# Issuing the first load of a streaming Lp-pooling kernel from the ScalarE queue instead of the SyncE queue

## The chip, the cores and the metric

The kernel runs on one core of one Trainium2 chip. The metric is the device time of one execution in microseconds (us); medians over several executions are given. A profile is one execution taken by the hardware profiler. Its span is about 2 us shorter than the device time, and its clock starts with the span. Engines are ACT (ScalarE), DVE (VectorE) and SP (SyncE, which here only issues DMAs); "the DMA engines" are the core's 16 engines that move the bytes.

## The reference

```python
batch, channels, length = 32, 256, 4096      # float32, p = 2, kernel_size = 4
for i in range(out_length):                  # out_length = length // 4
    window = np.abs(x[:, :, 4*i:4*i+4]) ** p
    result[:, :, i] = np.mean(window, axis=-1) ** (1.0 / p)
```

With p = 2, each output is the square root of the mean of four squares. The kernel reads 134.22 MB and writes 33.55 MB, and does very little arithmetic per byte.

## The kernel before

The input is cut into 32 blocks of 128 partitions x 8192 columns (4.19 MB each). For each half block ACT squares in place, DVE adds groups of four, and ACT takes the root of the result one step later. There are four input buffers. Three loads are issued ahead of the loop and a fourth at its start; each later load reuses a buffer and so has to wait for the reduces of the block four places ahead of it. Finished outputs leave from the ACT queue in groups of four blocks; two late groups are held back and leave from SP.

```python
in_pool = ctx.enter_context(tc.tile_pool(name="in_pool", bufs=4))

def load(i):
    xt = in_pool.tile([P, W], fp32)
    nc.sync.dma_start(out=xt, in_=x_block(i))
    xts[i] = xt

# ... root(i, c): Sqrt on ACT; after a group's last root, nc.scalar.dma_start of the group

for i in range(3):
    load(i)

pending = None
for i in range(n):                           # n = 32
    if i + 3 < n:
        load(i + 3)
    # ...
    for c in range(0, W, CH):                # two halves of 4096 columns
        xh = xts[i][:, c:c + CH]
        nc.scalar.activation(out=xh, in_=xh, func=mybir.ActivationFunctionType.Square)
        nc.vector.tensor_reduce(out=ots[gi][:, at:at + CH // k], in_=xh.rearrange("p (n j) -> p n j", j=k),
                                axis=mybir.AxisListType.X, op=mybir.AluOpType.add)
        if pending is not None:
            root(*pending)
        pending = (i, c)
```

## Time and profile before

| | before |
|---|---|
| device time, median (first 3 runs) | 395.74 us (395.67 to 395.85) |
| span of the profile | 393.7 us |
| bytes moved, mean rate | 167.79 MB, 426 GB/s |
| ACT busy, DVE busy | 75%, 72% |
| first Square starts | 12.87 us |
| Square of the last block starts | 373.62 us |

From the profile page of the kernel before, three parts: the utilization rows (busy tenths in 40 equal slices of the span, and GB/s), the DMA queues (q1 is SP's, q10 ACT's), and the chain of waits that ended last, by engine.

```profile
DVE  0399996739976399764988559866598846999992
ACT  1699987469883798828988189863998819999981
...
DMA  8999998999999999999999999999999999999997
GB/s 350 446 430 426 426 426 373 449 446 430 433 426 426 426 430 453 440 430 433 426 426 426 426 449 443 427 433 430 426 426 426 443 446 433 430 433 426 426 435 314
...
q1 hardware_dynamic: 4896, 141.56, 83.9%
q10 hardware_dynamic: 1008, 26.21, 15.5%
...
DMA 72%; ACT 17%; DVE 9%; SPq 0%; issue 0%; ACTq 0%
```

The DMA row is the one without gaps. ACT and DVE rest for a quarter of the span, so nothing they do is worth time unless it leaves the DMA engines without work.

The timeline of ACT at the start of the kernel before (start, duration, engine and line, operation; in brackets the idle time before it and what ended it):

```profile
12.87 7.12 ACT L108 ACTIVATE xt<-xt 128x4096 f32<-128x4096 f32 x2 [10.86 <-DMA xt<-in_x_dram]
...
22.57 3.62 ACT L108 ACTIVATE xt<-xt 128x4096 f32<-128x4096 f32 x1 [0.21 <-DMA xt<-in_x_dram]
...
32.28 3.62 ACT L108 ACTIVATE xt<-xt 128x4096 f32<-128x4096 f32 x1 [0.55 <-DMA xt<-in_x_dram]
...
42.00 3.62 ACT L108 ACTIVATE xt<-xt 128x4096 f32<-128x4096 f32 x1 [0.56 <-DMA xt<-in_x_dram]
```

Each block's first Square waits for a load, and the loads come 9.7 us apart. Now SP's timeline for load 4, the first one that must wait for a buffer:

```profile
25.29 0.33 SPq L79 DMA_DIRECT2D xt<-in_x_dram  x1
```

Load 4 is issued at 25.29 us. The load in front of it in the queue, load 3, lands at 42.0 us. I call the difference, 16.7 us, the lead: about that long could the issue come later before the queue ran empty.

### The profile page before, as it was taken

Reading aid. Unit: us, or ns where it says so; the run is one execution under the profiler, and the core shown is the slowest. Engines: PE = TensorE matmul, PEld = TensorE weight load, DVE = VectorE, ACT = ScalarE, POOL = GpSimd, SP = SyncE. Lnnn points to the kernel's source line nnn. Section 1 sums busy time; section 2 is a strip of 40 time slices with the busy share of each in tenths; the row PEclk is TensorE's granted clock in tenths of the full one; section 3 lists DMA queues with packets and bytes.
Section 4 is the critical chain, followed back from the end, with each engine's and each line's share of the span. In section 5 each row is a group of like instructions: output and inputs, shape, how many; then the busy total and the mean of one; then the engine's idle time right before and its main releaser. Section 6 shows DMA issues by size and latency. Waiting matters only on the chain.

```text
span 393.7 us, 357 instructions
## 1 busy us (share of the span) xinstructions
DVE 282.8 (72%) x64; ACT 294.7 (75%) x130; POOL 0.2 (0%) x4
## 2 busy tenths in 40 slices
DVE  0399996739976399764988559866598846999992
ACT  1699987469883798828988189863998819999981
POOL 0000000000000000000000000000000000000000
DMA  8999998999999999999999999999999999999997
GB/s 350 446 430 426 426 426 373 449 446 430 433 426 426 426 430 453 440 430 433 426 426 426 426 449 443 427 433 430 426 426 426 443 446 433 430 433 426 426 435 314
DMA packets 5906, 167.79 MB, mean 426 GB/s; under 512 B 656, under 2 KB 656, under 8 KB 656
## 3 DMA queue, kind: packets, MB, share of 16 engines
q1 hardware_dynamic: 4896, 141.56, 83.9%
q10 hardware_dynamic: 1008, 26.21, 15.5%
q14 instruction: 2, 0.02, 0.0%
HBM read 134.22 MB, written 33.55 MB: 426 GB/s over the span
## 4 chain that ended last, share of the span: by engine, by line
DMA 72%; ACT 17%; DVE 9%; SPq 0%; issue 0%; ACTq 0%
DMA xt<-in_x_dram 72%; ACT xt L108 14%; DVE ot L112 9%; ACT ot L87 2%; SPq L79 0%; ACTq L108 0%
## 5 line engine op out<-in xcount | busy, mean ns | idle before, releaser
L112 DVE TENSOR_REDUCE ot<-xt 128x1024 f32<-128x4096 f32 x64 | 282.8, 4420 | 103.4 <-ACT xt L108 102.6
L108 ACT ACTIVATE xt<-xt 128x4096 f32<-128x4096 f32 x64 | 230.9, 3610 | 87.6 <-DMA xt<-in_x_dram 85.0
L87 ACT ACTIVATE ot<-ot 128x1024 f32<-128x1024 f32 x64 | 67.0, 1047 | 4.2 <-DVE ot L112 3.4
L108 ACT ACT_TABLE_LOAD x1 | 1.3, 1283 | 0.7 <-PEq L139 0.7
L87 ACT ACT_TABLE_LOAD x1 | 1.3, 1283 | 0.0
L139 POOL MEMSET const-uint8-127<- 128x1 uint8 x1 | 0.1, 102 | 0.0
L139 POOL MEMSET const-bfloat16-1.0<- 128x1 bf16 x1 | 0.1, 101 | 0.0
L139 POOL MEMSET const-float32-0.0<- 128x1 f32 x1 | 0.1, 98 | 0.2 <-issue 0.2
L139 POOL MEMSET const-float32-1.0<- 128x1 f32 x1 | 0.1, 98 | 0.0
## 6 DMA issues: line engine op xcount, KB each, us to landing
xt<-in_x_dram SPq DMA_DIRECT2D x32, 4096.0 KB, 35.9
out_dram<-ot ACTq DMA_DIRECT2D x6, 4096.0 KB, 23.2
out_dram<-ot SPq DMA_DIRECT2D x1, 4096.0 KB, 34.1
out_dram<-ot SPq DMA_DIRECT2D x1, 3072.0 KB, 12.3
out_dram<-ot ACTq DMA_DIRECT2D x1, 1024.0 KB, 5.6
```

Source lines behind the costliest of these rows:

```text
L87: nc.scalar.activation(out=o, in_=o, func=mybir.ActivationFunctionType.Sqrt, scale=1.0 / k,)
L108: nc.scalar.activation(out=xh, in_=xh, func=mybir.ActivationFunctionType.Square,)
L112: nc.vector.tensor_reduce(out=ots[gi][:, at:at + CH // k], in_=xh.rearrange("p (n j) -> p n j", j=k), axis=mybir.AxisListType.X, op=mybir. ...
L139: nc = _bacc.Bacc("TRN2", target_bir_lowering=False, num_devices=1)
```

## The change

It puts the first load on another issuing queue. The intent is a quicker head: two sequencers issue in parallel at the start.

```diff
     def load(i):
         xt = in_pool.tile([P, W], fp32)
-        nc.sync.dma_start(out=xt, in_=x_block(i))
+        queue = nc.scalar if i == 0 else nc.sync
+        queue.dma_start(out=xt, in_=x_block(i))
         xts[i] = xt
```

## The prediction

> **What bounds the kernel now.** The DMA engines. The page's utilization rows show them at 90% or more in nearly every one of the 40 slices, 426 GB/s over the span (167.79 MB in 393.7 us), while DVE is busy 72% and ACT 75%. The chain of waits is DMA 72%. Load issues are early: load 4 leaves SP when the reduces of block 0 end, at 25.2 us, while loads 2 and 3 (9.7 us each, read from Squares starting at 12.87, 22.57 us in the timeline) still fill the SP queue until about 42 us. So SP's wait for DVE (293.7 us in the view of waits) costs nothing: there are about 17 us of slack. The last load lands at 373.5 us; two held stores then run under the last block's compute.
>
> **What changes.** No bytes and no work: one of SP's 32 load issues (about 0.4 us each) becomes ACT's first instruction, ahead of its 1.28 us table load. ACT then waits idle until 12.87 us anyway, so that costs nothing. Load 1 now leaves SP at 0.73 us, beside load 0 from ACT, not behind it.
>
> **Consequence.** The Trainium skill, "DMA: Bandwidth & Descriptors", section "Queues, rings and completion order", says that each of the 16 DMA engines goes round-robin between queues. This trace agrees: beside the first store, load 6 took 18.1 us (63.8 to 82.0) instead of 9.7. So loads 0 and 1 each get half the rate, and both land near 22 us. The first Square starts at about 22.5 us (range 20 to 23), not 12.87.
>
> **Critical share.** None of that delay should reach the end. From 22.5 us ACT runs back to back at 2 x (3.6 + 1.06) = 9.3 us a block, against 9.7 a load. Block 0's reduces end near 35 us, so load 4 is issued near 35; load 3 occupies the queue until 42. Load 5 goes near 44.8, before load 4 lands (51.7); load 6 near 54, before 61.5. Slack falls from about 17 to about 7 us but never to zero. The first store moves from 56.4 to about 64.7 us; the longer waits beside it (18 us) let ACT catch up by block 7, at about 91 us. After that the timeline is as before: bytes ahead of load 31 are the same, so it lands at 373.5 and the tail is unchanged. What may move is under 1 us: two queues starting together may fill the opening (the first 13 us moved about 400 GB/s, against 430 later), gaining up to 1 us.
>
> **Predicted:** 395.5 us, 80% range 394.3 to 396.7. Chances: faster by over 2% 0.005, within 2% 0.985, slower by over 2% 0.01.
>
> **What would show it.** Right: first Square near 22 us with Squares of blocks 0 to 3 then back to back; ACT's idle time before the first Square up by about 9.5 us, later idle before Squares down by as much; DMA utilization row unchanged, mean 426 GB/s; last load lands within 1 us of 373.5; SP's issue of load 4 near 35 us. Wrong: first Square near 13 us (no equal sharing), or a hole in DMA between 35 and 65 us (slack ran out), or the last landing moved.
>
> **What would make it wrong.** Unequal arbitration; loads from two queues running together faster or slower than one queue (no two loads on different queues overlap in this trace); the shifted store meeting loads so that a later block finds no load queued.

## The result and the profile after

| | before | after |
|---|---|---|
| device time, median of 6 runs | 395.71 us (395.51 to 395.85) | 395.45 us (395.34 to 395.53) |
| span of the profile | 393.7 us | 393.3 us |
| first Square starts | 12.87 us | 22.85 us |
| load 4 issued | 25.29 us | 35.27 us |
| first store issued | 56.38 us | 63.97 us |
| Square of block 7 starts | 91.64 us | 91.35 us |
| Square of the last block starts | 373.62 us | 373.26 us |

The ratio is 0.9994, with a 95% interval of 0.9981 to 1.0007: the same. A ratio is the mean time of one kernel's fast runs over that of the other's of the same rounds, so it is not quite the ratio of the medians quoted.

The same rows of the page of the changed kernel:

```profile
DVE  0039999995976499764988559866598846999992
ACT  1069999987883798828988189872998819999981
...
DMA  8999999999999999999999999999999999999997
GB/s 340 447 433 433 427 427 403 437 433 433 427 427 427 433 450 437 431 433 430 427 427 427 437 450 433 427 433 430 427 427 430 440 443 433 433 430 430 427 433 317
...
q1 hardware_dynamic: 4752, 137.37, 81.4%
q10 hardware_dynamic: 1152, 30.41, 18.0%
...
DMA 65%; ACT 21%; DVE 11%; issue 0%; ACTq 0%
```

ACT and DVE start a slice later and are then packed with 9s where they had gaps; from about the tenth slice on the digits are almost those of before. The DMA row has changed in a single digit, and 4.19 MB have moved from q1 to q10. ACT's timeline at the start:

```profile
0.73 0.40 ACTq L80 DMA_DIRECT2D xt<-in_x_dram  x1
1.16 1.28 ACT L109 ACT_TABLE_LOAD   x1 [1.16 <-PEq L140]
22.85 7.12 ACT L109 ACTIVATE xt<-xt 128x4096 f32<-128x4096 f32 x2 [20.40 <-DMA xt<-in_x_dram]
...
32.24 3.60 ACT L109 ACTIVATE xt<-xt 128x4096 f32<-128x4096 f32 x1
...
41.30 3.60 ACT L109 ACTIVATE xt<-xt 128x4096 f32<-128x4096 f32 x1
```

The load was issued at 0.73 us, as early as before, and yet the first Square waits 10 us longer. After that the Squares have no bracket: ACT no longer waits for loads, it is behind them. Counting the trace's DMA packets of 32 KB by the microsecond in which they started shows why (these are counts from the trace's DMA records, changed kernel):

```
us from         5   6   7   8   9  10  11  12  13  14
SP queue       10   0  16   0  12   4   1  15   0  15
ACT queue       1  15   0  16   0   5  11   0  16   0
```

The 16 engines take turns between the two queues. Loads 0 and 1 move at half rate each and land together, at 22.83 and 22.65 us. Now the waits of ACT for loads (total, times, longest), first before:

```profile
ACT xt L108 <- DMA xt<-in_x_dram: 85.0, 32, 10.9
```

and after:

```profile
ACT xt L109 <- DMA xt<-in_x_dram: 84.9, 26, 20.4
```

ACT waited for loads as long in total, to 0.1 us. It waited 9.5 us more ahead of the first Square, and six later waits vanished. SP's timeline after, for loads 4 and 5:

```profile
35.27 0.33 SPq L80 DMA_DIRECT2D xt<-in_x_dram  x1
44.78 0.33 SPq L80 DMA_DIRECT2D xt<-in_x_dram  x1
```

Load 3 landed at 42.1 us and load 4 at 51.8 us, so the leads are now 6.8 and 7.0 us. They shrank by the ten microseconds that the head lost, but they did not reach zero, and the DMA engines never noticed.

### The profile page after: what moved, and what is told of

The parts are those of the page before. It is cut to its first block, busy times and chain, and to the rows that moved or that the text cites. A ratio compares the mean times of both kernels' runs of the same rounds, so it can differ in the third digit from the quotient of the medians.

```text
span 393.3 us, 357 instructions
## 1 busy us (share of the span) xinstructions
DVE 282.8 (72%) x64; ACT 294.0 (75%) x130; POOL 0.2 (0%) x4
## 4 chain that ended last, share of the span: by engine, by line
DMA 65%; ACT 21%; DVE 11%; issue 0%; ACTq 0%
DMA xt<-in_x_dram 65%; ACT xt L109 18%; DVE ot L113 11%; ACT ot L88 3%; ACT L88 0%; ACTq L109 0%
## 5 line engine op out<-in xcount | busy, mean ns | idle before, releaser
L109 ACT ACTIVATE xt<-xt 128x4096 f32<-128x4096 f32 x64 | 230.8, 3608 | 87.4 <-DMA xt<-in_x_dram 84.9
```

## The experiments

My theory: the DMA engines bound the kernel; the second queue delays block 0 by 10 us because it lets load 1 share the engines with it; the delay is paid out of the lead of the later loads, and nothing of it reaches the end as long as the lead stays above zero. Rivals: the issuing queue does not matter at all, as the same engines do the work; the delay does cost, but an opening with two queues earns it back; the delay would be made up over the kernel whatever its size; the ACT queue itself is late.

Ten kernels were run, all with correct results. The first four share one chip and the same runs of the kernel before (395.65 us), the next four another call (395.56 us), the last two a third (395.62 us). All diffs are against the kernel before, cut to the lines that matter. I call a difference real where the 95% interval of the ratio leaves out 1.

### The changed kernel again

No edit.

> The changed kernel once more, to be compared on one chip with the three others of this call. Slack theory (DMA engines bound; a late first Square is paid from waiting that ACT and the load queue had to spare): first Square 22.8 us, last load's Square 373.3 us, time 395.4 us, 0.1 to 0.4 us under the kernel before. Rival (the difference between the kernels is noise only): ratio 1.000 within 0.0003.

Measured: 395.58 us, ratio 0.9997 (0.9984 to 1.0009); first Square at 22.83 us, last block's Square at 373.45 us. The first Square repeats to 0.02 us. The gain does not: 0.07 us between the medians here, 0.26 us the first time. So the rival, noise only, stands.

### The same delay with one queue

```diff
-    for i in range(3):
-        load(i)
+    for i in range(3):
+        tile_for(i)                  # buffers in the old order
+    for i in (1, 0, 2):
+        load(i)                      # all on nc.sync
```

> All loads on SP, but load 1 is issued ahead of load 0, so block 0 is as late as in the changed kernel without a second queue. Slack theory: first Square 22.5 us, ACT back to back until block 7, first store near 64 us, time within 0.5 us of the kernel before. Rival (the ten us of delay do cost, and the second queue earns them back): about 405 us. Of the 0.3 us gain: if it comes from where the first store falls, this run is 0.2 to 0.4 us faster than before; if it comes from two queues opening together, it equals the kernel before within 0.1 us.

Measured: 395.41 us, ratio 0.9997 (0.9983 to 1.0011). The first Square starts at 22.48 us and load 4 is issued at 34.90 us. So a delay of 10 us costs nothing without any second queue, and the rival that a second queue earns it back falls. On the 0.3 us question the median alone agrees with "where the first store falls", but the ratio's interval includes 1 and settles nothing.

### Two queues without the delay

```diff
+        if i == 0:
+            for queue, c in ((nc.scalar, 0), (nc.sync, CH)):
+                queue.dma_start(out=xt[:, c:c + CH], in_=x_block(i)[:, c:c + CH])
+        else:
+            nc.sync.dma_start(out=xt, in_=x_block(i))
```

> Load 0 cut into two column halves, one from ACT and one from SP; loads 1 on from SP. Two queues open together as in the changed kernel, but block 0 is not held up by load 1. Sharing theory (what delays block 0 is load 1 running beside it at equal rate): first Square 12.5 to 13.5 us. Rival (a load on the ACT queue lands late by itself): later than 14 us. Time within 0.5 us of before; if the 0.3 us gain comes from two queues opening together it is 0.2 to 0.4 us faster, if from where the first store falls it equals the kernel before within 0.1 us.

Measured: 395.58 us, ratio 1.0 (0.9988 to 1.0013); first Square at 13.05 us. Here ACT issues half of block 0 at 0.73 us and block 0 is on time: what made it late in the changed kernel was not ACT's queue but another load beside it. Opening two queues together gains nothing measurable.

### All four opening loads from ACT

```diff
-        nc.sync.dma_start(out=xt, in_=x_block(i))
+        queue = nc.scalar if i < 4 else nc.sync
+        queue.dma_start(out=xt, in_=x_block(i))
```

> The four opening loads all leave from ACT, the others from SP. In the changed kernel the ACT queue's first packet starts at 3.51 us and the SP queue's at 1.75 us, though both were issued at 0.73 us. If the ACT queue starts late by its nature, the first packet is at 3.5 us, first Square at 14.6 us, and as the DMA engines bound the kernel the time rises by 1.5 to 2 us. If it was late only because SP issued beside it, first packet at 1.75 us, first Square at 12.9 us, time within 0.4 us of before. Sharing theory in both cases: no 22 us landing, although load 0 is on the ACT queue, as nothing runs beside it.

Measured: 397.68 us (396.33 to 398.04), ratio 1.0048 (1.0034 to 1.0062). Half of the expectation held: the ACT queue's first packet starts at 1.75 us and the first Square at 12.81 us, so ACT's queue is not late by nature. The time did not hold: it is 2.0 us over before, and neither theory had said that for an on-time first packet. SP's timeline of this run and ACT's first Squares of blocks 2 and 3 show what began at load 4, the first one from SP:

```profile
25.23 42.96 SPq L80 DMA_DIRECT2D xt<-in_x_dram  x4
...
35.88 3.62 ACT L109 ACTIVATE xt<-xt 128x4096 f32<-128x4096 f32 x1 [4.21 <-DMA xt<-in_x_dram]
...
55.31 3.62 ACT L109 ACTIVATE xt<-xt 128x4096 f32<-128x4096 f32 x1 [10.27 <-DMA xt<-in_x_dram]
```

Load 4 from SP runs beside loads 2 and 3 from ACT. Block 2 is 3.6 us late, and load 3 lands at 55.3 instead of 42.0 us, behind load 4 (49.2 us). That by itself only shares the engines. But later in this kernel the 16 completion increments of one load come further apart. A load counts as landed when the last of the 16 has come (I take each to be one engine's; no view names the engine); the spread between the first and the last of them, from the trace, was:

```
load that lands at about (us)        22.5     36     142     346    376
kernel before                        0.48    0.48   0.51    1.18   1.16
four opening loads on ACT            0.43    1.65   2.83    3.33   3.58
```

(The columns are the nearest load in each kernel.) The second column is not yet the start of it: loads 5 and 6 (61.4 and 71.1 us) are back at 0.44 us. The lasting spread opens with load 7 (1.5 us) and load 9 (3.0 us). Of the last load, twelve of the 16 increments have come by 373.12 us, earlier than the last one in the kernel before (373.53 us), but the sixteenth comes at 375.77 us. So the loss of 2.0 us sits in the last few increments. What put them behind is not shown. My own theory offers a candidate that I did not test: as block 3 was late, load 7, which reuses its buffer, was issued at 67.86 us, only 3.2 us before load 6 landed. That lead by itself cost nothing at first, as 41.5 MB had gone through by 100 us in both kernels. The next experiment on the spread is the last one below.

### Twenty microseconds of delay

```diff
+    for i in (1, 2, 0):              # buffers in the old order, as above
+        load(i)                      # then load(3); all on nc.sync
```

> All on SP, issued in the order 1, 2, 0, 3: block 0 lands third, first Square at 32.3 us, 20 us later than before. Slack theory: block 0's reduces end near 44.8 us, load 4 is issued then, but load 3 landed at 42 us and the queue is empty; load 4 lands near 56.8 us instead of 51.7, time plus 3.5 to 5.5 us (399.2 to 401.2). Rival (ACT and DVE have waits enough over the whole kernel, so any delay of the head is made up later): within 0.5 us of before. Rival (delay costs in full): plus 20 us.

Measured: 401.62 us, ratio 1.0153 (1.0138 to 1.0168), 6.1 us over before and 0.4 us above my range. The first Square starts at 32.12 us. The utilization rows of this run, in which the fifth slice is the hole:

```profile
DMA  9999599999999999999999999999999999999997
GB/s 368 420 420 443 210 404 410 404 420 437 443 433 420 433 443 437 421 433 437 437 427 424 440 440 430 421 440 433 433 424 440 437 433 424 430 437 433 433 429 329
```

SP's timeline of this run, loads 4 and 5:

```profile
44.54 0.33 SPq L84 DMA_DIRECT2D xt<-in_x_dram  x1
54.05 0.33 SPq L84 DMA_DIRECT2D xt<-in_x_dram  x1
```

Load 3 had landed at 41.8 us. The last packet of load 3 ended at 41.37 us and the first of load 4 started at 45.49 us: 4.1 us without a packet. Both the rival that any delay is made up and the rival that it costs in full fall.

### Twenty-nine microseconds of delay

```diff
+    for i in (1, 2, 3, 0):           # buffers in the old order, as above
+        load(i)                      # all on nc.sync
```

> All on SP in the order 1, 2, 3, 0: block 0 lands fourth, first Square at 42.0 us, 29 us later than before. Slack theory: load 4 is issued near 54.5 us with the queue empty since 42 us, lands near 66.4 us, plus 13.5 to 15.5 us (409 to 411.5): each microsecond of delay beyond the slack is paid in full. Rival (made up later): within 1 us of before. Rival (delay costs in full): plus 29 us.

Measured: 411.17 us, ratio 1.0395 (1.0379 to 1.041), 15.6 us over before; the time is inside my range, the difference 0.1 us above it. The first Square starts at 41.95 us, load 4 is issued at 54.38 us, and one whole slice of the DMA row is empty:

```profile
DMA  8999069999999999999999999999999999999998
```

### Three buffers, first load on SP, and on ACT

Both kernels have three input buffers and two loads ahead; the second has the change on top.

```diff
-    in_pool = ctx.enter_context(tc.tile_pool(name="in_pool", bufs=4))
+    in_pool = ctx.enter_context(tc.tile_pool(name="in_pool", bufs=3))
-    for i in range(3):
+    for i in range(2):
-        if i + 3 < n:
-            load(i + 3)
+        if i + 2 < n:
+            load(i + 2)
```

> The kernel before with three input buffers (two loads ahead of the loop, two ahead in it). Slack theory: slack is now about 7 us (load 3 issued at 25.3 us, load 2 lands at 32.3 us), still more than none: time within 0.7 us of before, 395.2 to 396.4. Rival (four buffers are already needed in full): plus 2 us or more.

Measured: 395.57 us, ratio 0.9999 (0.9983 to 1.0016). Load 3, now the first that waits for a buffer, is issued at 25.22 us and load 2 lands at 32.2 us: a lead of 7.0 us is enough.

> The same three buffers with load 0 on the ACT queue. Slack theory: load 0 lands at 22.8 us, load 3 is issued near 35.2 us, but load 2 landed at 32.4 us; load 3 lands near 47.2 us instead of 42, so this is slower than b3_sp by 3.5 to 6 us: the change that was free with four buffers is not with three. Rival (moving one issue to another queue never matters, as the same 16 engines do the work): equal to b3_sp within 0.5 us.

Measured: 402.04 us, ratio 1.0168 (1.0152 to 1.0183), that is 6.5 us over the same kernel with the first load on SP, and a little over my range. Load 3 is issued at 35.23 us, after load 2 has landed at 32.3 us. The stage in question in the two kernels (the view by stretches; columns: stretch and its length, DVE, ACT and POOL busy time with counts, granted clock, DMA share, GB/s), first with SP, then with ACT:

```profile
30.00:37.00 7.00, 6.12 (x3) 6.41 (x5) 0.00 (x0) 1.00 1.04 449
```

```profile
30.00:37.00 7.00, 6.37 (x3) 6.99 (x5) 0.00 (x0) 1.00 0.41 145
```

This is the same one-line change, and here it costs 1.6%. The rival that the issuing queue never matters falls.

### The opposite: an earlier start

```diff
+        if i == 0:
+            for queue, c in ((nc.sync, 0), (nc.sync, CH)):
+                queue.dma_start(out=xt[:, c:c + CH], in_=x_block(i)[:, c:c + CH])
```

> The opposite of the change: load 0 in two column halves, both on SP, one after the other, so that the first Square can start on half a block. Slack theory: first Square near 7.5 to 8 us instead of 12.9, and nothing gained at the end, time within 0.4 us of before. Rival (the head is on the critical path, an earlier start of compute is worth its time): about 5 us faster.

Measured: 395.32 us, ratio 0.9999 (0.9986 to 1.0011). The first Square starts at 8.00 us and the last block's at 373.57 us. ACT's timeline of this run:

```profile
8.00 3.62 ACT L112 ACTIVATE xt<-xt 128x4096 f32<-128x4096 f32 x1 [5.99 <-DMA xt<-in_x_dram]
...
12.89 3.62 ACT L112 ACTIVATE xt<-xt 128x4096 f32<-128x4096 f32 x1 [1.27 <-DMA xt<-in_x_dram]
...
22.60 3.62 ACT L112 ACTIVATE xt<-xt 128x4096 f32<-128x4096 f32 x1 [3.73 <-DMA xt<-in_x_dram]
```

Compute that starts 4.9 us earlier just waits longer for load 1. The head is off the critical path in both directions, as long as the lead lasts.

### One load from ACT in mid stream

```diff
+        queue = nc.scalar if i == 5 else nc.sync
```

> Load 5 alone from the ACT queue, opening in mid stream beside loads 3 and 4 on SP. It asks about the run with four loads on ACT, which took 2.0 us more although its first Square was on time and in which the 16 completion increments of one load spread over 1.5 us from load 2 on and 3 us later, against 0.5 us in the kernel before. Drift theory (a second load queue that opens in mid stream puts the 16 engines out of step, and each load lands with the last of them): spread over 1 us from load 3 on, time 0.5 to 2.5 us over before. Rival (the cost of that run lies in ACT issuing four loads, or in the queue change at load 4 alone): spread near 0.5 us as before, time within 0.3 us of before.

Measured: 395.56 us, ratio 1.0001 (0.9987 to 1.0014); spread 0.41 us at load 3, 0.40 us at loads 4 and 5 and 1.31 us at the end. The drift theory, as I had put it, falls: in this run a second load queue that opens in mid stream did not put the increments out of step. But load 5 passed load 4: it landed at 57.6 us, load 4 at 61.3 us (63.8 and 51.7 us in the kernel before). The lead stayed long here (load 7 was issued 15.1 us before load 6 landed), so this run does not test the short lead named above. What put the last increments behind with four loads on ACT stays open.

### The runs side by side

Lead is the time from the issue of the first load that waits for a buffer to the landing of the load in front of it; a negative one is an empty queue. Costs are differences of medians from the kernel before; for the changed kernel the first six runs are used, and for three buffers on ACT the difference from three buffers on SP. The run with four loads on ACT is left out: its first SP load has no load in front of it in its queue, and its cost is not explained.

| kernel | first Square, us | lead, us | cost, us |
|---|---|---|---|
| before | 12.87 | 16.7 | 0 |
| after | 22.85 | 6.8 | -0.3 |
| one queue, order 1, 0, 2 | 22.48 | 7.0 | -0.2 |
| three buffers, SP | 12.79 | 7.0 | 0.0 |
| one queue, order 1, 2, 0 | 32.12 | -2.7 | 6.1 |
| three buffers, ACT | 22.81 | -2.9 | 6.5 |
| one queue, order 1, 2, 3, 0 | 41.95 | -12.4 | 15.6 |

Down to a lead of 6.8 us, delay is free in these runs. With an empty queue the cost is the length of the emptiness plus 3.2 to 3.6 us (6.1 - 2.7 = 3.4, 6.5 - 2.9 = 3.6, 15.6 - 12.4 = 3.2). In the order 1, 2, 0, about 1 us of this is the time from an issue into an empty queue to its first packet (44.54 to 45.49 us), and 0.4 us lies between load 3's last packet and its landing (41.37 to 41.80 us). Another 0.9 us is load 5: it was issued only 2.5 us before load 4 landed, and landed 10.6 us after it (56.54 to 67.17 us); in the changed kernel, with leads near 7 us, these two landings are 9.7 us apart (51.80 to 61.51 us). That the short lead is the reason is argued, not tested, and the rest, about 1 us, is not attributed. I had left load 5's part out of my ranges.

## Why the prediction was right

The time alone would prove little, as "no change" also follows from the rival that the queue does not matter. What decides are the marks in the trace that were forecast, and the runs that took the lead away.

- **The bound.** Right: the DMA row and the rate hardly changed (one digit; 426 and 427 GB/s), and an earlier start (half of block 0 first) gained nothing.
- **Equal sharing.** Right: predicted first Square at 22.5 us (20 to 23), measured 22.85; packets of the two queues alternate. The Trainium skill, "DMA: Bandwidth & Descriptors", section "Queues, rings and completion order", has the round-robin, and this trace agrees. The run with halves on two queues shows that it was load 1, not ACT's queue, that delayed block 0.
- **The lead.** Right: load 4 predicted near 35 us, measured 35.27; load 5 near 44.8, measured 44.78; load 6 near 54, measured 53.83; first store near 64.7, measured 63.97. Slack was to fall from about 17 to about 7 us and measured 16.7 and 6.8. The runs with 20 and 29 us of delay and with three buffers show that this slack was really what paid: where it ended, the cost began.
- **The recovery.** Right: the idle time before the first Square rose by 9.5 us, the total did not (85.0 and 84.9), and by block 7 (91.35 against 91.64 us) the delay is gone.
- **A possible gain of up to 1 us from two queues filling the opening.** Not borne out. By the trace's packets, 8.39 MB had gone through at 22.08 us before and at 22.25 us after: the opening was not faster. ACT's first packet started at 3.51 us though issued at 0.73 us; it starts at 1.75 us when SP issues nothing beside it (the run with four loads on ACT). The prediction's "about 400 GB/s" for the first 13 us was a loose reading: by stretches it is 363 in both kernels, and 417 and 419 when counted from 1.75 us. In the pair of profiles the changed kernel gets ahead only around the first store, between 24 MB (58.35 and 58.40 us) and 33.5 MB (81.30 and 81.10 us). But three buffers on SP and the halves on two queues, which leave the first store where it was (issued at 56.30 us with three buffers), also start the last block's Square 0.2 us earlier (373.40 and 373.38 us). So the 0.3 us is not attributed: the interval of the ratio includes 1 in each of these runs, and I call it noise until shown otherwise.

## What to carry to other kernels

In a kernel bound by DMA like this one, the time at which compute starts is worth nothing by itself; what counts is that each load is issued while enough older loads are still queued, so read the lead (issue of the first load that waits for a buffer against the landing of the load in front of it) before judging any change of the head. The second queue added no rate here (426 and 427 GB/s); it changed which load was served when. The first load, which had nothing in front of it, did not start sooner on ACT (3.51 against 1.75 us), but now shared the engines with load 1. Load 5, moved in mid stream, passed load 4 and made that one 9.6 us late. So before moving a load, ask what it will then run beside and who waits for that. The same line was free with a lead of 16.7 us to spend and cost 6.5 us with 7.0 us.

## What the Trainium skill lacked or had wrong

- "DMA: Bandwidth & Descriptors", section "Issuing engines are not separate DMA queues", says that initiating DMAs on several engines only saves sequencer time. The runs show that it also changes which load arrives first: block 0 landed at 22.83 instead of 12.85 us, and with three buffers this cost 6.5 us.
- The same page, section "Latency and other measured facts", gives about 0.6 us to the first byte on this path. With idle engines the trace agrees if one counts from the end of the issuing instruction: 0.6 us (1.11 to 1.75 us; 1.0 us from its start). What the page lacks is the same time beside other loads. Counted from the start of the issue it is 2.8 us for ACT's load issued together with SP's (0.73 to 3.51 us), and 4.1 us for a store issued beside loads (105.99 to 110.06 us).
- No page that I read says how far ahead of the queue's end a load must be issued. Here 6.8 us was enough, and with 2.5 us the load landed 10.6 us after the one in front of it, not 9.7 us.
- No page that I read gives a figure for the spread between the 16 completion increments of one load over a long stream: 0.5 us early and 1.2 us late in the kernel before, up to 3.6 us at the last load with four opening loads on ACT, whose cause is open.
